# A hybrid decoder layer on one core: where DeltaNet's outputs are scaled, and when sums of weight blocks are formed

## The chip, the cores and the metric

One Trainium2 chip, one core, one launch. The metric is the device time of the launch in microseconds, the median of several executions. Everything is float32 in and out.

## The reference, cut to what matters

512 tokens of width 1024 go through two token mixers, retention and a gated DeltaNet; their outputs are merged under sigmoid gates, projected, and followed by a gated MLP with a short convolution.

```python
u = rmsnorm(h, g_mix)
rq, rk, rv, rgate, dq, dk, dv, dz, db, da, gate_r, gate_d = split(u @ w_in)
ro = groupnorm(retention_chunkwise(rotary(rq), rotary(rk) / 8, rv)) * ret_norm_g
y_ret = (silu(rgate) * ro) @ w_ret_br
q, k, v = silu(causal_dwconv([dq, dk, dv]));  q, k = l2norm(q), l2norm(k)
def step(S, (u_n, w_n, q_n, k_n, a_n, d_n)):      # chunks of 128 tokens, per head
    v_new = u_n - w_n @ S
    o = q_n @ S + a_n @ v_new
    S = S * d_n + k_n.T @ v_new
    return S, o
y_dn = (rmsnorm(scan(step)) * silu(dz)) @ w_dn_br
h = h + (sigmoid(gate_r) * y_ret + sigmoid(gate_d) * y_dn) @ w_o
a, b = split(causal_dwconv(rmsnorm(h) @ w_up) + ffn_conv_b)      # 2816 wide each
h = h + (silu(a) * b) @ w_down
return rmsnorm(h)
```

Both mixers have 8 heads; with chunks of 128 each DeltaNet head makes four steps of its scan.

## The kernel before

**Matmuls and weights.** Each product is made of three: operands are split into a high and a low part, and `mm3` adds hi x hi, hi x lo and lo x hi. SyncE fetches weights in order into four raw buffers `wraw` (`fetch`). For each block `weights` lets ACT cast `whi` and DVE subtract `wlo`; there are four buffers of each. A block's buffer comes free when it is split, so fetching goes on as ACT and DVE go on.

**Fewer products, sums of weights.** Six matrices, numbered 0 to 5 (gate_d, gate_r, w_dn_br, w_ret_br, then OUT = 4, the out projection, and DOWN = 5), are multiplied as 2 x 2 blocks with seven products instead of eight. Four of the seven take sums of weight blocks: s1 = w21 + w22, s3 = w11 + w21, s2 = w11 + s1, s4 = w12 + s2 (`SUMS`). The sums are formed in DRAM. `presum` has POOL issue, for each, one DMA that copies the first block (`s<-wm`, `s<-wd`) and later one that adds the second into it; where the second is itself a sum, its row reads `s<-s`. So s4 <- s2 may only start when s2 <- s1 has landed. `presums` spreads these DMAs over the program: for each, `pace` lets ACT write a tiny `tick`, which POOL copies to `tock`; this ties the DMA to a place in ACT's program. Each DMA of matrices 0 to 4 moves 1 MB; DOWN's are cut into four parts of 704 KB. Matrices 0 to 2 are spread over the scans; 3 and OUT follow in `late_sums`, which starts once the last head's triangular inverse is made; DOWN's 32 DMAs are spawned ahead of the out projection.

**The operands' side.** The left operands need sums too. `combine_c` makes them from `r` (or `u`, `d`): POOL subtracts into `ry`, DVE's `rz<-ry,r` and `rz<-rz,r` go on from there, then `parts_of` casts `oh` on ACT and subtracts `ol` on DVE. A matrix's results collect in `res`; POOL multiplies a finished `res` of matrix 2 by its gate (`res<-res,res`), and on matrix 3 they are transposed (`pmt`) and become the out projection's operands `mr`, `mt`, `mB`, `mT` (`m_out`; `mt1` on POOL). The residual `h` is fetched by SyncE (L1345) in eight DMAs ahead of matrix 3's weights.

**Who sets the order.** All instructions are written by one Python program in one pass, and the order of writing is the order on each engine. The class `Order` keeps a clock that each matmul moves forward (`product`), and for each engine the time at which it is free by a table of costs (`issue`). Work beside the matmuls is a generator, `spawn`ed with a delay; after each matmul `poll` resumes those whose time has come, and after its step a generator is due at the planned end of what it wrote plus `HOP` = 0.3 us. So a planned time that changes anywhere changes the order written from there on.

**The scan.** `scan` is one such generator per head. For chunk n it writes on PE `psc<-Sn,k` (state times keys), on DVE `R`, on PE `psc<-R,tt`, on ACT `vn`; on PE `psc<-vn,ktok` into quarter 3 of a PSUM bank and `psc<-Sn,q`, `psc<-vn,gb` into quarter 2 of the same bank; then on DVE the new state `Sn` from quarter 3, and on ACT the scaled output `o` from quarter 2. Four heads run in the first scan (about 190 to 275 us of the profile), four in the second (400 to 450).

After the branch matrices (to about 625 us) come the out projection, the normalised `u2`, the up projection with its convolution (products `pa`, `pb`), and from 927 us the down projection (`pd`).

Of the kernel before, what the change touches and what calls it, by code (L numbers as in the profile page):

```python
# [14 lines left out]
ALU = mybir.AluOpType  # L15
PSUM = bass.MemoryType.PSUM
# [42 lines left out]
OUT, DOWN = 4, 5  # L59
INNER = (HK, HK, HK, HK, HK, NK)  # L60
# [3 lines left out]
SUMS = (("s1", "w21", "w22"), ("s3", "w11", "w21"), ("s2", "w11", "s1"), ("s4", "w12", "s2"))  # L64
# [33 lines left out]
class Order:  # L98
# [6 lines left out]
    def __init__(self):  # L105
        self.clock = 0.0
        self.free = {}
        self.tasks = []
        self.n = 0
        self.now = None  # L110
        self.done = None

    def issue(self, engine, us):
        at = self.clock if self.now is None else self.now
        self.done = self.free[engine] = max(self.free.get(engine, 0.0), at) + us

    def product(self, us):
        self.clock += us
# [2 lines left out]
    def spawn(self, gen, after=0.0):  # L121
        self.n += 1
        heapq.heappush(self.tasks, ((self.clock if self.now is None else self.now) + after, self.n, gen))
# [41 lines left out]
class Engine:  # L165
# [7 lines left out]
    def __getattr__(self, op):  # L173
        f = getattr(self.engine, op)

        def call(out, *args, **kw):
            aps = [a for a in (*args, *kw.values()) if isinstance(a, bass.AP)]
            n = math.prod((args[0] if op == "bn_stats" else out).shape[1:])
            if op == "dma_start":
                aps = []  # L180
            ptrs = sum(a.free_size() == 1 for a in aps) if n > 1 else 0
            us = self.cost(op, n, ptrs, aps[0].space if aps else None)
            if "accum_out" in kw:
                us += 0.09 - 0.055 * (self.name == "act")
            if self.name == "vec" and any(a.tensor.name == self.last for a in aps):
                us += 0.125
            self.last = None if op == "dma_start" else out.tensor.name
            if len(args) > 1 and args[1] in TABLES and args[1] != self.table:
                self.table = args[1]
                us += 1.3  # L190
            self.order.issue(self.name, us)
            return f(out, *args, **kw)  # L192

        return call
# [19 lines left out]
def body(nc, tc, ctx, io):  # L214
    sp = nc.sync
    order = Order()
    spawn, poll, hold = order.spawn, order.poll, order.hold
    vec = Engine(order, "vec", nc.vector, vec_cost)
    act = Engine(order, "act", nc.scalar, act_cost)
    pool = Engine(order, "pool", nc.gpsimd, pool_cost)  # L220
# [10 lines left out]
    late = []  # L231
# [3 lines left out]
    def S(name, dt=F32):  # L235
        return heap.tile([P, T], dt, name=name, tag="s", bufs=HEAP)
# [4 lines left out]
    def s4(name, n=4, bufs=16):  # L241
        return mini.tile([P, n], F32, name=name, tag=f"n{n}", bufs=bufs)

    def PS(name):
        return psp.tile([P, T], F32, name=name, tag="ps")

    def v3(ap, n=4):
        return ap.rearrange("p (n f) -> p n f", n=n)

    def bc(ap, f=P):  # L250

        return ap.unsqueeze(2).to_broadcast([ap.shape[0], ap.shape[1], f])

    def ck(n, f=P):
        return slice(n * f, (n + 1) * f)
# [25 lines left out]
    sums = {(s, n): dram.tile([P, 512 * INNER[s] + 64], F32, name=f"{n}_{s}") for s in range(DOWN + 1) for n, _, _ in SUMS}  # L281

    def quarter(s, name):
        if name not in WD:
            assert (s, name) in made
            return sums[s, name]
        return (io["wd"] if s == DOWN else io["wm"][s])[WD[name]]

    made = set()

    def presum(s, parts):


        n = 512 * INNER[s] // parts
        for add in range(2):
            for name, a, b in SUMS:
                for i in range(parts):
                    c = ck(i, n)
                    kw = dict(accum_op=ALU.add) if add else {}
                    pool.dma_start(sums[s, name][:, c], quarter(s, b if add else a)[:, c],  # L300
                                        max_dma_last_dim=2048, **kw)
                    if add and i == parts - 1:
                        made.add((s, name))
                    yield

    def pace():

        tick = const.tile([P, 1], F32, name="tick", tag="tick", bufs=2)
        tock = const.tile([P, 1], F32, name="tock", tag="tock", bufs=2)
        act.copy(tick, ones[:, :1])  # L310
        pool.tensor_scalar(tock, tick, 1.0, None, ALU.mult)

    def presums(ss, parts, *times):

        todo = (None for s in ss for _ in presum(s, parts))
        for start, end, n in times:
            for i in range(n):
                while order.clock < start + (end - start) * i / n:
                    yield 0.5
                pace()  # L320
                if next(todo, 0) == 0:
                    return
                yield
# [163 lines left out]
    def rsqrt(out, ms):  # L487
        pool.tensor_tensor(out, ms, mhalf[:, :out.shape[1]], ALU.pow)
# [31 lines left out]
    def transpose4(src, name):  # L520
        pt = PS(name)
        for n in range(NT):
            pe.transpose(pt[:, ck(n)], src[:, ck(n)], ident)
        return pt
# [221 lines left out]

    spawn(clear(), 30.0)

    spawn(presums(range(3), 1, (110.0, 325.0, 24)), 30.0)
    a_dram = [dram.tile([4, GH, NT, 32, 32], F32, name=f"a_dram{g}") for g in range(2)]  # L750
    x_dram = [dram.tile([4, GH, NT, 32, 32], F32, name=f"x_dram{g}") for g in range(2)]
    R32 = [ck(b, 32) for b in range(4)]
# [170 lines left out]
    def scan(hd, i):  # L923
        h = hd["h"]
        o = S(f"o{h}")
        ssqo = s4("ssqo")
        st = None
        for n in range(NT):
            c = ck(n)
            ps = v3(PS("psc"))  # L930
            R = hd["vtok"][:, c]
            if n > 0:
                pe.matmul(ps[:, 0], hd["kT"][:, c], st, start=True, stop=True)
                yield
                R = small.tile([P, P], F32, name="R", tag="R", bufs=5)
                vec.scalar_tensor_tensor(R, ps[:, 0], hd["c2"][:, n:n + 1], hd["vtok"][:, c], ALU.mult, ALU.add)
                yield
            pe.matmul(ps[:, 1], tts[i][:, n], R, start=True, stop=True)
            yield
            vn = small.tile([P, P], F32, name="vn", tag="vn", bufs=5)  # L940
            act.copy(vn, ps[:, 1])
            yield
            if n < NT - 1:
                pe.matmul(ps[:, 3], hd["ktok"][:, c], vn, start=True, stop=True)
            if n > 0:
                pe.matmul(ps[:, 2], hd["qT"][:, c], st, start=True, stop=False)
            pe.matmul(ps[:, 2], hd["attn"][:, c], vn, start=(n == 0), stop=True)
            yield
            if n < NT - 1:
                sn = small.tile([P, P], F32, name="Sn", tag="Sn", bufs=8)  # L950
                if n == 0:
                    vec.tensor_copy(sn, ps[:, 3])
                else:
                    vec.scalar_tensor_tensor(sn, st, egl[:, h, n:n + 1], ps[:, 3], ALU.mult, ALU.add)
                st = sn
            act.activation(o[:, c], ps[:, 2], AF.Identity, scale=hd["rqs"][:, n:n + 1])
            spawn(scan_ssq(o[:, c], ssqo[:, n:n + 1]), 0.4)
            yield
        yield 0.8
        ms = s4("mso")  # L960
        vec.tensor_scalar(ms, ssqo, 1.0 / P, EPS, ALU.mult, ALU.add)
        r = s4("ro")
        yield
        rsqrt(r, ms)
        yield
        vec.tensor_tensor(v3(o), v3(o), bc(r), ALU.mult)
        hd["got"].add("o")
        yield PW
        pt = transpose4(o, "pot")
        yield  # L970
        d = S(f"doT{h}")
        act.activation(d, pt, AF.Identity, scale=prm[:, P_DG:P_DG + 1])
        doT[h] = d

    def scan_ssq(o, ssq):
        junk = small.tile([P, P], F32, name="junk", tag="junk", bufs=2)
        act.activation(junk, o, AF.Square, accum_out=ssq)
        yield
# [239 lines left out]
    def late_sums():  # L1218
        while "up" not in heads[H - 1]["got"]:
            yield 0.5  # L1220
        for s in (3, OUT):
            yield from presums((s,), 1, (order.clock, order.clock + 65.0, 8))

    for src, raw, x in ((roT, rr_, "r"), (doT, dd, "d")):
        if x == "d":
# [120 lines left out]
        matrix(s, opnd)  # L1346


    spawn(presums((DOWN,), 4, (order.clock, order.clock + 230.0, 32)))
    u2hi = [S(f"u2hi{k}", F32R) for k in range(KT)]  # L1350
    u2lo = [S(f"u2lo{k}", F32R) for k in range(KT)]
    ssqs = [s4("ssq1", 2) for _ in range(NT)]
# [49 lines left out]
    product(1, o_get, HK, [[(full, C[t], True, o_into(t, 0, C[t], ALU.add, True))] for t in range(2)])  # L1402
    product(6, o_get, HK, [[(full, A[t], False, o_into(t, 1, A[t], ALU.subtract, True))] for t in range(2)], tail=2)
    u2 = (u2hi, u2lo)


    def ffn_conv(ps, ci):
# [11 lines left out]
    f_raw, act_raw, parts = {}, {}, {}  # L1419
# [55 lines left out]
    at = [0]  # L1475
# [155 lines left out]
```

## Time and profile before

| | |
|---|---|
| median of three executions | 1037.42 us (1036.62 to 1039.86) |
| the profiled execution | 1040.07 us, span 1038.3 us, mean granted clock 0.981 |
| TensorE busy | 994.5 us, 96% |
| VectorE, ScalarE, GpSimd busy | 739.4, 536.8, 208.8 us |
| moved by DMA | 189.29 MB, 182 GB/s |

The profile is of one execution, whose own time lies 2.65 us above the median. Engines are PE (TensorE), PEld (its weight loads), DVE (VectorE), ACT (ScalarE), POOL (GpSimd) and SP (SyncE). A row such as `wlo<-wraw,whi` names what is written and from what, by the program's names. Instructions written through the recording helper all carry its line, L192 (L207 for matmuls, L211 for transposes, L274 for fetches of weights), so they are told apart by their names.

### The profile page before, as it was taken

Reading aid. Unit: us, or ns where it says so; the run is one execution under the profiler, and the core shown is the slowest. Engines: PE = TensorE matmul, PEld = TensorE weight load, DVE = VectorE, ACT = ScalarE, POOL = GpSimd, SP = SyncE. Lnnn points to the kernel's source line nnn. Section 1 sums busy time; section 2 is a strip of 40 time slices with the busy share of each in tenths; the row PEclk is TensorE's granted clock in tenths of the full one; section 3 lists DMA queues with packets and bytes.
Section 4 is the critical chain, followed back from the end, with each engine's and each line's share of the span. In section 5 each row is a group of like instructions: output and inputs, shape, how many; then the busy total and the mean of one; then the engine's idle time right before and its main releaser. Section 6 shows DMA issues by size and latency. Waiting matters only on the chain.

```text
span 1038.3 us, 14387 instructions
## 1 busy us (share of the span) xinstructions
PE 994.5 (96%) x5241; PEld 826.9 (80%) x5241; DVE 739.4 (71%) x1332; ACT 536.8 (52%) x1132; POOL 208.8 (20%) x252
## 2 busy tenths in 40 slices
PE   8999999999899999899994989999999999999997
PEld 7888888787688887778883868788888888888886
DVE  5867796665677795466787959966565576678785
ACT  5599221367645323566764545555444433346664
POOL 3022112123333122331523200231112121000001
PEclk9999999999999999999998989999999999999999
DMA  6343569747658633259997665856589988336663
GB/s 241 98 144 112 172 186 221 216 130 158 181 161 181 151 104 100 103 165 283 323 314 191 220 225 170 274 185 220 186 197 197 206 173 182 100 113 201 197 186 125
DMA packets 82230, 189.29 MB, mean 182 GB/s; under 512 B 22704, under 2 KB 31216, under 8 KB 82160
## 3 DMA queue, kind: packets, MB, share of 16 engines
q1 hardware_dynamic: 54640, 123.36, 36.3%
q0 software_dynamic: 27520, 65.02, 28.2%
q8 instruction: 41, 0.67, 0.3%
q14 instruction: 29, 0.24, 0.1%
HBM read 185.17 MB, written 68.19 MB: 244 GB/s over the span
## 4 chain that ended last, share of the span: by engine, by line
PE 83%; DVE 7%; ACT 4%; DMA 3%; issue 2%; POOL 1%; SPq 0%; POOLq 0%; DVEq 0%; ACTq 0%
PE pb L207 12%; PE pa L207 11%; PE py L207 11%; PE pd L207 10%; PE pr L207 9%; PE pz L207 8%; PE pq L207 4%; PE pv L207 4%; PE pk L207 4%; PE psc L207 2%; DVE wlo L192 2%; PE po L207 2%; DMA wraw<-s 1%; PE pm L207 1%; PE pro L207 1%
## 5 line engine op out<-in xcount | busy, mean ns | idle before, releaser
L192 DVE TENSOR_TENSOR wlo<-wraw,whi 128x1024 fp32r<-128x1024 f32 x212 | 260.0, 1229 | 70.9 <-ACT whi L192 70.4
L192 ACT CAST whi<-wraw 128x1024 fp32r<-128x1024 f32 x212 | 219.4, 1035 | 157.8 <-PE pr L207 55.9
L192 POOL TENSOR_SCALAR tock<-tick 128x1 f32<-128x1 f32 x72 | 33.3, 462 | 423.4 <-ACT tick L192 423.2
L207 PE MATMUL py<-wlo,oh 128*128 128x512 f32 x160 | 64.0, 400 | 12.3 <-DVE wlo L192 12.3
L192 DVE SCALAR_TENSOR_TENSOR acc<-pb,prm,acc 128x511 f32<-128x511 f32 (+1 forms) x44 | 33.0, 749 | 57.1 <-ACT acc L192 56.4
L207 PE MATMUL pa<-u2lo,whi 128*128 128x512 f32 (+1 forms) x192 | 71.7, 373 | 1.8 <-DVE u2lo L192 1.8
L207 PE MATMUL pa<-u2hi,whi 128*128 128x512 f32 (+1 forms) x192 | 71.6, 373 | 0.0
L207 PE MATMUL pa<-u2hi,wlo 128*128 128x512 f32 (+1 forms) x192 | 71.3, 371 | 0.0
L207 PE MATMUL pb<-u2hi,whi 128*128 128x512 f32 (+1 forms) x184 | 70.0, 380 | 0.0
L207 PE MATMUL pb<-u2lo,whi 128*128 128x512 f32 (+1 forms) x184 | 69.9, 380 | 0.0
L207 PE MATMUL pb<-u2hi,wlo 128*128 128x512 f32 (+1 forms) x184 | 69.9, 380 | 0.0
L207 PE MATMUL py<-whi,oh 128*128 128x512 f32 x160 | 64.4, 403 | 1.1 <-ACT res L192 1.1
L207 PE MATMUL py<-whi,ol 128*128 128x512 f32 x160 | 63.8, 399 | 0.0
L207 PE MATMUL pd<-whi,T 128*128 128x512 f32 (+1 forms) x198 | 55.4, 366 | 0.0
L207 PE MATMUL pz<-uhi,whi 128*128 128x512 f32 x128 | 52.5, 410 | 0.0
L207 PE MATMUL pr<-whi,uhi 128*128 128x512 f32 x128 | 51.7, 404 | 0.0
L207 PE MATMUL pz<-uhi,wlo 128*128 128x512 f32 x128 | 50.3, 393 | 0.0
L207 PE MATMUL pz<-ulo,whi 128*128 128x512 f32 x128 | 50.3, 393 | 0.0
L207 PE MATMUL pr<-whi,ulo 128*128 128x512 f32 x128 | 50.1, 391 | 0.0
L207 PE MATMUL pr<-wlo,uhi 128*128 128x512 f32 x128 | 49.9, 390 | 0.0
L192 DVE SCALAR_TENSOR_TENSOR acc<-pa,prm,acc 128x511 f32<-128x511 f32 (+1 forms) x44 | 33.0, 749 | 19.0 <-ACT acc L192 18.2
L207 PEld LDWEIGHTS py<-wlo,oh 128*128 128x128 f32 x160 | 31.0, 194 | 19.4 <-DVE wlo L192 12.7
(320 smaller groups left out, 2515.1 us busy)
## 6 DMA issues: line engine op xcount, KB each, us to landing
wraw<-w SPq DMA_DIRECT2D x100, 512.0 KB, 4.5
s<-wm POOLq DMA_DIRECT2D x30, 1024.0 KB, 8.8
wraw<-s SPq DMA_DIRECT2D x60, 512.0 KB, 4.4
s<-wd POOLq DMA_DIRECT2D x24, 704.0 KB, 5.5
wraw<-wm SPq DMA_DIRECT2D x30, 512.0 KB, 5.0
s<-s POOLq DMA_DIRECT2D x10, 1024.0 KB, 11.7
wraw<-wd SPq DMA_DIRECT2D x15, 512.0 KB, 3.7
s<-s POOLq DMA_DIRECT2D x8, 704.0 KB, 9.2
```

The source lines that it names most:

```text
L192: return f(out, *args, **kw)
L207: self.engine.matmul(out, lhsT, rhs, start=start, stop=stop, **kw)
```

## The change

It has four parts.

1. `Order.issue` is given the PSUM banks of an instruction's operands, and plans it no earlier than `HOP` after the planned end of another engine's use of the same bank. This holds for the whole program, so instructions of ACT, DVE and PE change places in many spots, each by a few rows.
2. `scan` yields between DVE's `Sn` and ACT's `o`: `o` is planned behind the state, and so is the head's next chunk.
3. `presum` takes several matrices at once. The last sum, s4 <- s2, of each is written after the first two DMAs (copies) of the next matrix, and that of the last matrix at the very end. The times follow: for matrices 0 to 2 23 DMAs over 110 to 318 us of the planner's clock and one at 330, instead of 24 over 110 to 325; in `late_sums` 15 over 125 us and one 15 us later, instead of twice 8 over 65 us.
4. DOWN's 32 sums are spawned behind the out projection, over 200 us, instead of ahead of it, over 230 us.

```diff
-    def issue(self, engine, us):
+    def issue(self, engine, us, banks=()):
         at = self.clock if self.now is None else self.now
-        self.done = self.free[engine] = max(self.free.get(engine, 0.0), at) + us
+        at = max(at, self.free.get(engine, 0.0))
+        for b in banks:
+            at = max([at, *(t + self.HOP for e, t in self.banks.get(b, {}).items() if e != engine)])
+        self.done = self.free[engine] = at + us
+        for b in banks:
+            self.banks.setdefault(b, {})[engine] = self.done
...
-            self.order.issue(self.name, us)
+            banks = {a.tensor.name for a in (out, *aps) if a.space == PSUM} if op != "dma_start" else ()
+            self.order.issue(self.name, us, banks)
...
-    def presum(s, parts):
-        n = 512 * INNER[s] // parts
-        for add in range(2):
-            for name, a, b in SUMS:
-                for i in range(parts):
-                    ...
+    def presum(ss, parts):
+        todo, late = [], []
+        for s in ss:
+            steps = [(s, name, i, q) for add in (1, 2) for name, *src in SUMS for i in range(parts) for q in (src[add - 1],)]
+            steps = [(*x, n >= len(steps) // 2) for n, x in enumerate(steps)]
+            todo += steps[:2 * parts] + late + steps[2 * parts:-parts]
+            late = steps[-parts:]
+        for s, name, i, q, add in todo + late:
+            ...
...
-    spawn(presums(range(3), 1, (110.0, 325.0, 24)), 30.0)
+    spawn(presums(range(3), 1, (110.0, 318.0, 23), (330.0, 330.0, 1)), 30.0)
...
                 st = sn
+                yield
             act.activation(o[:, c], ps[:, 2], AF.Identity, scale=hd["rqs"][:, n:n + 1])
...
-        for s in (3, OUT):
-            yield from presums((s,), 1, (order.clock, order.clock + 65.0, 8))
+        c = order.clock
+        yield from presums((3, OUT), 1, (c, c + 125.0, 15), (c + 140.0, c + 140.0, 1))
...
-    spawn(presums((DOWN,), 4, (order.clock, order.clock + 230.0, 32)))
...
     product(6, o_get, HK, [[(full, A[t], False, o_into(t, 1, A[t], ALU.subtract, True))] for t in range(2)], tail=2)
     u2 = (u2hi, u2lo)
+    spawn(presums((DOWN,), 4, (order.clock, order.clock + 200.0, 32)))
```

The number of instructions of each kind stays as it was. Three places show what moves. The first is POOL during matrix 2, where OUT's last two sums were issued. `s_4_95` and `s_4_96` are OUT's s2 and s4 in both programs; before, the rows are

```order
L192 DMA s_4_95<-s_4_93 128x4x512
L192 TENSOR_TENSOR ry_5596<-r_3871,r_3693 128x256
L192 TENSOR_TENSOR ry_5596<-r_3693 128x256
L192 TENSOR_SCALAR tock<-tick 128x1
L192 DMA s_4_96<-s_4_95 128x4x512
L192 TENSOR_TENSOR ry_5622<-r_3913,r_3743 128x256
L192 TENSOR_TENSOR ry_5646<-r_3953,r_3787 128x256
L192 TENSOR_TENSOR ry_5622<-r_3743 128x256
L192 TENSOR_TENSOR res_5568<-res_5568,res_4834 128x512
L192 TENSOR_TENSOR ry_5646<-r_3787 128x256
L192 TENSOR_TENSOR res_5573<-res_5573,res_4845 128x512
L192 TENSOR_TENSOR ry_5669<-r_3995,r_3829 128x256
```

and now

```order
L200 TENSOR_SCALAR tock<-tick 128x1
L200 DMA s_4_95<-s_4_93 128x4x512
L200 TENSOR_TENSOR ry_5639<-r_3789 128x256
L200 TENSOR_TENSOR ry_5666<-r_3997,r_3831 128x256
L200 TENSOR_TENSOR res_5568<-res_5568,res_4845 128x512
L200 TENSOR_TENSOR ry_5666<-r_3831 128x256
L200 TENSOR_TENSOR res_5743<-res_5743,res_4976 128x512
L200 TENSOR_TENSOR res_5751<-res_5751,res_4981 128x512
L200 TENSOR_TENSOR res_5691<-res_5691,res_4934 128x512
L200 TENSOR_TENSOR res_5696<-res_5696,res_4939 128x512
L200 TENSOR_SCALAR tock<-tick 128x1
L200 DMA s_4_96<-s_4_95 128x4x512
```

The last sum, `s_4_96<-s_4_95`, stood with only two `ry` between it and the sum that it reads; all the other `ry` and `res` stood behind it. Now the `ry` and `res` stand ahead of it, and it comes after the last `res` pair.

The second is the place of that last sum's `tick` on ACT, during matrix 2's last products. Before, ACT had there

```order
L192 CAST oh<-ry_5646 128x512
L192 CAST whi<-wraw 128x1024
L192 CAST oh<-ry_5669 128x512
L192 CAST whi<-wraw 128x1024 x5
L192 ACTIVATE res_5950<-py 128x512
L192 ACTIVATE res_5955<-py 128x512
L192 CAST whi<-wraw 128x1024 x3
L192 COPY mr_6022<-pmt 128x512
L192 CAST mB_6029<-mr_6022 128x512
```

and now it has

```order
L200 CAST oh<-ry_5639 128x512
L200 CAST whi<-wraw 128x1024
L200 CAST oh<-ry_5666 128x512
L200 CAST whi<-wraw 128x1024 x2
L200 COPY tick<-ones 128x1
L200 CAST whi<-wraw 128x1024 x3
L200 ACTIVATE res_5950<-py 128x512
L200 ACTIVATE res_5955<-py 128x512
L200 CAST whi<-wraw 128x1024 x3
L200 COPY mr_6022<-pmt 128x512
L200 CAST mB_6029<-mr_6022 128x512
```

The `tick` of the last sum has come between the second and the third of five casts of weights; the casts themselves keep their order.

The third is DVE in the first scan, at the last states of heads 2 and 3 (`Sn`), with the retention's `ro` and `sT`. Before:

```order
L192 SCALAR_TENSOR_TENSOR k_2482<-pk,prm,k_2482 128x509
L192 TENSOR_SCALAR ro<-pro,mv,rgn 128x128 x4
L192 TENSOR_TENSOR wlo<-wraw,whi 128x1024
L192 TENSOR_TENSOR sT<-prs,cst 128x512 x2
L192 TENSOR_TENSOR o_2124<-o_2124,ro 128x512
L192 SCALAR_TENSOR_TENSOR Sn<-Sn,egl,psc 128x128 x2
L192 COPY rS<-pkv 128x128
L192 SCALAR_TENSOR_TENSOR R<-psc,c_1032,vtok_1168 128x128
L192 SCALAR_TENSOR_TENSOR R<-psc,c_1208,vtok_1301 128x128
```

Now:

```order
L200 SCALAR_TENSOR_TENSOR Sn<-Sn,egl,psc 128x128
L200 TENSOR_SCALAR ro<-pro,mv,rgn 128x128 x4
L200 TENSOR_SCALAR ssk<-ssk 128x4
L200 TENSOR_SCALAR ro<-pro,mv,rgn 128x128 x4
L200 TENSOR_TENSOR sT<-prs,cst 128x512 x2
L200 TENSOR_TENSOR c_2610<-beta,rk 128x4
L200 TENSOR_TENSOR sr<-c_2610,rk 128x4
L200 SCALAR_TENSOR_TENSOR c_2611<-sr,eG 128x4
L200 SCALAR_TENSOR_TENSOR A_2523<-pkk,sr,gb_2269 128x128 x4
L200 SCALAR_TENSOR_TENSOR R<-psc,c_1032,vtok_1168 128x128
L200 COPY rS<-pkv 128x128
L200 SCALAR_TENSOR_TENSOR Sn<-Sn,egl,psc 128x128
```

The two `Sn` stood as a pair behind `ro`, `wlo`, `sT` and the normalised outputs `o`; now one stands ahead of `ro` and the other behind `ro`, `sT` and the first instructions of head 4's `A`, close behind its `R`.

More of the change, by code (lines that the diff above doesn't have):

```diff
@@ L107, in __init__ @@
         self.free = {}
+        self.banks = {}
         self.tasks = []
@@ L289, in body @@
     made = set()
-    def presum(s, parts):
-        n = 512 * INNER[s] // parts
-        for add in range(2):
-            for name, a, b in SUMS:
-                for i in range(parts):
[L298 to L304, printed above, removed]
+    def presum(ss, parts):
[6 more added lines that the diff above has]
+        for s, name, i, q, add in todo + late:
+            c = ck(i, 512 * INNER[s] // parts)
+            kw = dict(accum_op=ALU.add) if add else {}
+            pool.dma_start(sums[s, name][:, c], quarter(s, q)[:, c], max_dma_last_dim=2048, **kw)
+            if add and i == parts - 1:
+                made.add((s, name))
+            yield
     def pace():
@@ L313, in presums @@
     def presums(ss, parts, *times):
-        todo = (None for s in ss for _ in presum(s, parts))
+        todo = presum(ss, parts)
         for start, end, n in times:
@@ L955, in scan @@
                 st = sn
+                yield
             act.activation(o[:, c], ps[:, 2], AF.Identity, scale=hd["rqs"][:, n:n + 1])
```

## The prediction

> **What bounds the kernel now.** I read the page first: which engine is full, and what the chain that ended last is made of.
>
> ```profile
> PE 994.5 (96%) x5241; PEld 826.9 (80%) x5241; DVE 739.4 (71%) x1332; ACT 536.8 (52%) x1132; POOL 208.8 (20%) x252
> PE 83%; DVE 7%; ACT 4%; DMA 3%; issue 2%; POOL 1%; SPq 0%; POOLq 0%; DVEq 0%; ACTq 0%
> ```
>
> TensorE is busy for 994.5 of 1038.3 us. The change takes no matmul away, so only the other 43.8 us, and the stretches in which TensorE runs at a lower clock, can give time. So the waits of PE come next: who was waited for, us in total, times, the longest.
>
> ```profile
> PE py L207 <- DVE wlo L192: 12.3, 1, 12.3
> PE psc L207 <- DVE Sn L192: 5.4, 3, 3.1
> PE pmt L211 <- DVE res L192: 3.9, 1, 3.9
> PE pvt L211 <- ACT v L192: 3.1, 1, 3.1
> PE po L207 <- DVE wlo L192: 2.3, 1, 2.3
> PE psc L207 <- DVE R L192: 2.0, 2, 1.4
> ```
>
> One wait of 12.3 us is the largest by far; the three rows of the scans make 10.5 us. Third, busy time and granted clock around each, to see what a wait leaves behind it (columns: window, its length, busy us and count of PE, PEld, DVE, ACT, POOL, then PE's clock, the DMA engines' busy share, GB/s).
>
> ```profile
> 235.40:240.40 5.00, 4.81 (x22) 4.28 (x23) 1.31 (x5) 4.77 (x13) 0.00 (x0) 0.66 0.50 179
> 266.00:271.00 5.00, 5.00 (x33) 3.71 (x34) 4.47 (x9) 4.40 (x10) 1.02 (x2) 0.66 0.81 149
> 430.00:435.00 5.00, 4.62 (x20) 4.15 (x21) 1.92 (x8) 2.97 (x13) 0.61 (x2) 0.66 0.23 93
> ...
> 558.10:570.40 12.30, 0.03 (x1) 0.00 (x0) 9.00 (x7) 3.12 (x5) 7.85 (x9) 0.62 0.54 97
> 570.40:575.00 4.60, 4.57 (x12) 3.62 (x13) 4.57 (x7) 2.37 (x5) 0.00 (x0) 0.54 0.61 195
> 575.00:602.80 27.80, 27.80 (x123) 22.71 (x121) 21.30 (x22) 12.11 (x15) 7.05 (x4) 1.00 0.74 259
> 602.80:606.70 3.90, 0.04 (x1) 0.00 (x0) 3.71 (x6) 2.21 (x3) 0.00 (x0) 0.82 0.56 184
> 606.70:612.10 5.40, 5.35 (x16) 4.38 (x17) 4.16 (x5) 1.99 (x3) 0.00 (x0) 0.50 0.54 163
> ```
>
> A wait costs twice: itself, and the clock after it. After the 12.3 us it stands at 0.54 over 4.60 us (4.60 x 0.46 = 2.1 us lost), after the 3.9 us at 0.50 over 5.40 (2.7), in the three scan windows at 0.66 over 5.00 (1.7 each, about 1.5 in the last, which holds some idle time: 4.9). So 14.4 us are at stake at 570 and 15.4 in the scans.
>
> **The sums of the matrices.** Fourth, what ended the 12.3 us: the rows of POOL, DVE and PE there (start, duration, what, and the idle time before with its releaser).
>
> ```profile
> 542.36 1.30 POOL L192 DMA_DIRECT2D s<-s  x1 [0.37 <-issue]
> ...
> 548.92 0.21 POOL L192 TENSOR_SCALAR tock<-tick 128x1 f32<-128x1 f32 x1 [3.79 <-ACT tick L192]
> ...
> 559.24 1.30 POOL L192 DMA_DIRECT2D s<-s  x1 [10.10 <-DMA wraw<-s]
> 560.07 1.90 POOL L192 TENSOR_TENSOR ry<-r,r 128x256 f32<-128x256 f32 x2
> ...
> 565.91 1.18 POOL L192 TENSOR_TENSOR ry<-r 128x256 f32<-128x256 f32 x1
> ```
>
> ```profile
> 561.33 6.05 DVE L192 SCALAR_TENSOR_TENSOR rz<-ry,r 128x256 f32<-128x256 f32 x1 [7.23 <-POOL ry L192]
> 567.42 0.42 DVE L192 SCALAR_TENSOR_TENSOR rz<-rz,r 128x256 f32<-128x256 f32 x1
> ...
> 569.15 1.22 DVE L192 TENSOR_TENSOR wlo<-wraw,whi 128x1024 fp32r<-128x1024 f32 x1
> ```
>
> OUT's last sum, s4 <- s2, stands next on POOL at 548.92, but reads s2, whose own second half was issued at 542.36; it goes out at 559.24, 16.9 us later. (The named releaser, a transfer of SyncE, is only the last one that the profile saw; the sum has no need of it.) Behind it, in order, stand `ry` and `res`; DVE's `rz` waits for the `ry`, `wlo` stands behind `rz`, and PE waits for `wlo`. The change moves this sum far back: on POOL its place falls behind all of these, so the wait on s2 is gone (s2 has then had some 49 us). I take the whole 14.4 us away and ask what is late next. DVE's `rz` took 6.05 us where its twin took 0.42, while POOL's `ry` and `res` ran. That POOL work stays and now runs from about 549; DVE has wlo, two `ol`, a `res` to do before it. Residual: nothing if POOL is done by then, 3.5 us if `rz` is blocked in one piece of a few POOL instructions; I take 1.5, nearer to nothing, since they start 10 us earlier.
>
> By the Trainium skill ("SBUF — State Buffer", section "SBUF: two separate sides") the pair of ports that VectorE shares with GpSimd is an exclusive lock whose loser blocks for whole instructions. The 6.05 us beside 0.42 agree; the rule speaks against this change, since the POOL work is only moved and blocks wherever it lands: by it I would put 3.5 in place of 1.5, and the sum 2 us higher.
>
> Where does the sum go? On ACT its `tick` now stands between two `whi` casts, those that ran at 585.65 and 588.37, and on POOL behind the last `res` pair:
>
> ```profile
> 587.10 3.52 POOL L192 TENSOR_TENSOR res<-res,res 128x512 f32<-128x512 f32 x2 [2.97 <-DVE res L192]
> ```
>
> ```profile
> 588.37 1.06 ACT L192 CAST whi<-wraw 128x1024 fp32r<-128x1024 f32 x1 [1.67 <-PE py L207]
> ...
> 601.87 2.17 ACT L192 CAST whi<-wraw 128x1024 fp32r<-128x1024 f32 x2 [6.03 <-DMA wraw<-s]
> ```
>
> ```profile
> 589.92 3.88 SPq L1345 DMA_DIRECT2D h<-x  x8
> 594.11 14.07 SPq L274 DMA_DIRECT2D wraw<-s  x6
> ...
> 622.77 0.33 SPq L274 DMA_DIRECT2D wraw<-s  x1
> ```
>
> So it is issued at about 591 of the old time: exactly when SyncE fetches the eight `h`, and just ahead of the weights for which ACT already waited 6.03 us, DVE's `res` behind it, and PE 3.9 us. Its price: in a quieter window two such accumulating transfers moved 2.10 MB (first row) and took 74.2% of 16 engines over 17 us, 12.6 us, so 6.3 us for one of 1 MB; by the queue's mean over the kernel (28.2% of 1038.3 us for 65.02 MB, 4.5 us a MB) it is 4.7. The third row is how long such a sum takes to land.
>
> ```profile
> q0 software_dynamic: 1056, 2.10, 74.2%
> ```
>
> ```profile
> q0 software_dynamic: 27520, 65.02, 28.2%
> s<-s POOLq DMA_DIRECT2D x10, 1024.0 KB, 11.7
> ```
>
> Between 0 (the transfer stretches and leaves the engines to the weights) and +6.3 (all of it ahead of the weights) I take +4.7, since the weights there were late already. SyncE wants s4 itself only for the second product on OUT, whose first fetch goes out at 622.77 (last row of SyncE above); landing 11.7 us after 591, or 20 in the crowd, it is there. The sums of the first three matrices move too, with nothing of PE behind POOL there: 0.
>
> **The scans.** ACT's `o` now stands behind DVE's `Sn` in the plan, and the planner knows of banks. On the chip much of this already held:
>
> ```profile
> ACT o L192 <- DVE Sn L192: 24.4, 16, 6.2
> ```
>
> In 16 of 24 steps `o` waited for `Sn` anyway. What moves is who waits behind `o` (ACT's `vn`, casts and `k`), and how the scan's matmuls fall between the others. The longest wait, ended by this row, comes from DVE's order: the last `Sn` of heads 2 and 3 stand as a pair behind `wlo`, `sT` and `o`.
>
> ```profile
> 233.40 1.29 DVE L192 TENSOR_TENSOR sT<-prs,cst 128x512 f32<-128x512 f32 x2
> 234.59 0.69 DVE L192 TENSOR_TENSOR o<-o,ro 128x512 f32<-128x512 f32 x1
> 235.19 0.61 DVE L192 SCALAR_TENSOR_TENSOR Sn<-Sn,egl,psc 128x128 f32<-128x128 f32 x2
> ```
>
> In the new order one of them comes ahead of `ro` and `sT`, the other behind them. That place is worth 3.1 + 1.7 = 4.8; I take -4. The ends: all 15.4 away, or +5, one such place more. For the 2.0 and 3.1 us of the other rows I see the same instructions ahead as before (`uz` ahead of `Sn` at 430, `gb` ahead of `v`), so they stay.
>
> The windows of 430 and 235 show the clock falling after waits of at most 2.3 (5.4 less 3.1) and 3.1 us. By the Trainium skill ("TensorE: Matmul & The Clock Gate", section "What's actually happening") it falls after an idle window of about 3.4 us that runs freely; the shorter waits here were followed by the lower clock all the same, so the rows decide; by the rule the place would be worth 3.1 instead of 4.8.
>
> **The out and the down projection.** DOWN's sums start behind the out projection: eight transfers of 704 KB leave it, and the two `mt` of POOL run earlier. PE's 2.3 us there follow this:
>
> ```profile
> 648.84 3.40 DVE L192 SCALAR_TENSOR_TENSOR mt<-mt,mr 128x512 f32<-128x512 f32 x1
> ```
>
> DVE's `mt` took 3.40 us beside POOL's. The block moves with POOL's `mt`; DVE is full there and the weights are not what PE waits for. Taken as 0, with -2.3 (the wait gone) and +2.3 (another as long) as ends. In the up projection all 32 fall into 200 us instead of 230 us begun earlier:
>
> ```profile
> 687.17:926.88 239.71, 239.71 (x1123) 201.23 (x1122) 151.56 (x221) 98.78 (x157) 36.16 (x51) 1.00 0.69 174
> ```
>
> PE has no gap at all there and the DMA engines are 0.69 busy; eight more transfers of 0.72 MB at 4.5 us a MB are 26 us of 240, so 0.80. Free: the cover is that share below 1 and the buffers of weights ahead. If it went, PE would wait for `whi`.
>
> The bank rule also moves a few instructions at the start and shifts the last transposes of `u2` behind about nine matmuls: +0.5, between -1.9 and +1.9, which is nine times the 0.21 us of a matmul in the row above (239.71 us over 1123).
>
> **The sum.** Against the profiled execution, 1040.07 us (span 1038.3): -14.4 + 1.5 + 4.7 - 4 + 0 + 0.5 = -11.7, so 1028.4. That execution lies 2.65 above the median 1037.42 of the three runs, which I take off: 1025.7.
>
> **Rivals.** (1) Given back: the residual is 3.5, the late sum costs 6.3 and the scans nothing: -14.4 + 3.5 + 6.3 + 0.5 = -4.1, so 1033.3. For it: the DMA engines' crowd at 591 and POOL's block. Beside it stands a rule of the Trainium skill ("DMA: Bandwidth & Descriptors", section "SWDGE vs HWDGE vs iDMA"): every DMA engine takes turns between the software and the hardware queue, so the sum would get its half at once; only the run can show it. (2) Hidden: residual and collision 0, the scans give back half of 15.4: -14.4 - 8 = -22.4, so 1015.0. For it: s4 is wanted only 31 us later, and a transfer behind a full queue may simply stretch. (3) The scans' part does nothing, since ACT waited anyway: -7.7, so 1029.7. (4) Slower: with the planner putting each scan's next matmul and `o` later, the chain of a head grows. If `o`, 0.37 us, comes into each of 24 steps, that is 8.9 us, and two more halved windows make 12.3; with the -7.7 of the rest, +4.6, so 1042.0. It decides once the scans lose over 10.8 us (7.7 and the bound of 3.1). Against it: PE has other matmuls between the scans' steps.
>
> **How the numbers follow.** 0.3%, about what a measurement of this kernel can tell from no change, is 3.1 us: faster is below 1034.3, slower above 1040.5. Forecast 0.42, rival 3 0.15, rival 1 0.15 (a fifth of it beyond 1034.3), rival 2 0.17, rival 4 0.06, an unforeseen small loss 0.05, mostly within 0.3%. So faster 0.84, same 0.09, slower 0.07. The range runs from rival 2, 1014, to just past rival 1, 1035, and leaves out 0.2. The forecast's own range is 1021 to 1029.
>
> **What would show it.** PE's row "py <- DVE wlo" falls from 12.3 to under 4; the releaser of POOL's last `s<-s` is a tick, and nothing waits behind it; ACT's wait for `wraw<-s` near 590 grows from 6.0 to 8 to 12 us, PE's "pmt <- DVE res" with it; the scan rows fall from 10.5 to about 7; the up projection stays without gaps. It is wrong if the 12.3 us go to another wait of the branch matrices, if the scans' rows grow, or if PE waits for `whi` in the up projection.

## The result: 1028.16 us, and the profile after

The changed kernel takes 1028.16 us (median of four, 1027.78 to 1029.33) against 1037.39: a ratio of 0.9909, 95% interval 0.989 to 0.9927. The forecast was 1025.7. The profiled execution took 1027.94 us with a span of 1026.1; before it was 1040.07, so the two profiles are 12.1 us apart and the medians 9.2. The sum was made between profiles and came to -11.7.

The sum came out nearly right, and its terms did not. The waits of PE after the change (who was waited for, us in total, times, longest):

```profile
PE pmt L219 <- DVE res L200: 8.8, 1, 8.8
PE py L215 <- DVE wlo L200: 7.2, 2, 5.5
PE pm L215 <- DMA tt<-x_dram: 2.5, 1, 2.5
...
PE psc L215 <- DVE R L200: 1.7, 2, 1.2
```

The 12.3 us are gone, but 7.2 us of the same wait stay, and the wait for `res` has grown from 3.9 to 8.8: the two together were 16.2 us and are 16.0. Of the scans' 10.5 us only 1.7 are left, and a wait of 2.5 us for the transfer `tt<-x_dram` is new. To see what each stage is worth, take the first and last start of groups of PE's matmuls, the last two numbers before the semicolon; first the kernel before, then after.

```profile
L207 PE MATMUL pz<-uhi,whi x128: 387/390/774, 335.1 to 457.2; 128*128 128x512 f32 x128
L207 PE MATMUL py<-whi,oh x160: 388/389/775, 468.8 to 634.3; 128*128 128x512 f32 x160
L207 PE MATMUL po<-whi,mT x64: 387/389/629, 647.8 to 681.5; 128*128 128x512 f32 x64
L207 PE MATMUL pd<-whi,T x198: 278/389/398, 956.6 to 1031.7; 128*128 128x512 f32 x154, 128*128 128x256 f32 x44
```

```profile
L215 PE MATMUL pz<-uhi,whi x128: 388/390/504, 332.0 to 448.1; 128*128 128x512 f32 x128
L215 PE MATMUL py<-whi,oh x160: 387/390/775, 460.3 to 623.5; 128*128 128x512 f32 x160
L215 PE MATMUL po<-whi,mT x64: 387/390/506, 637.3 to 668.3; 128*128 128x512 f32 x64
L215 PE MATMUL pd<-whi,T x198: 278/389/398, 944.4 to 1019.5; 128*128 128x512 f32 x154, 128*128 128x256 f32 x44
```

Start and first scan, to the first `pz`: 335.1 to 332.0, -3.1 us. The second scan, first to last `pz`: 122.1 to 116.1, -6.0. The branch matrices, last `pz` to last `py`: 177.1 to 175.4, -1.7. The out projection, last `py` to last `po`: 47.2 to 44.8, -2.4. From there to the last `pd`: 350.2 to 351.2, +1.0. The matrices, where the change to the sums aims, gave only 1.7 us.

**What is left of the 12.3 us.** POOL and DVE where the stall was, after the change:

```profile
548.08 1.24 POOL L200 TENSOR_TENSOR ry<-r 128x256 f32<-128x256 f32 x1
548.77 1.23 POOL L200 TENSOR_TENSOR ry<-r,r 128x256 f32<-128x256 f32 x1
549.45 1.76 POOL L200 TENSOR_TENSOR res<-res,res 128x512 f32<-128x512 f32 x1
550.67 1.22 POOL L200 TENSOR_TENSOR ry<-r 128x256 f32<-128x256 f32 x1
```

```profile
548.20 4.79 DVE L200 TENSOR_TENSOR wlo<-wraw,whi 128x1024 fp32r<-128x1024 f32 x1
...
554.29 1.22 DVE L200 TENSOR_TENSOR wlo<-wraw,whi 128x1024 fp32r<-128x1024 f32 x1
```

POOL no longer waits for the sum there. It computes until 551.89, and the `wlo` that PE wants lasts 4.79 us, from POOL's first `ry` to just behind its last, instead of 1.22. The shorter of the two waits, 1.7 us, follows a `wlo` of the same kind: 4.87 us at 536.86, beside five `ry` of POOL.

**Where the sum went.** ACT, POOL, SyncE and PE around the fetch of `h` (issued from 575.07 to 578.98), and how long the transfers of this window took to land:

```profile
591.58 1.04 ACT L200 CAST whi<-wraw 128x1024 fp32r<-128x1024 f32 x1 [10.87 <-DMA wraw<-s]
```

```profile
576.89 1.30 POOL L200 DMA_DIRECT2D s<-s  x1
```

```profile
575.07 3.91 SPq L1357 DMA_DIRECT2D h<-x  x8
```

```profile
596.46 1.11 PE L219 MATMUL pmt<-cst,res 128*128 128x128 f32 x4 [8.76 <-DVE res L200]
```

```profile
wraw<-s SPq DMA_DIRECT2D x6, 512.0 KB, 12.6
h<-x SPq DMA_DIRECT2D x8, 256.0 KB, 5.8
s<-s POOLq DMA_DIRECT2D x1, 1024.0 KB, 15.6
```

ACT's wait for weights grew from 6.03 to 10.87 us and PE's from 3.91 to 8.76. The sum itself is issued at 576.89, in the middle of the fetch of `h`.

### The profile page after: what moved, and what is told of

Read it like the earlier page. It is cut to its first block, busy times and chain, and to the rows that moved or that the text cites. A ratio compares the mean times of both kernels' runs of the same rounds, so it can differ in the third digit from the quotient of the medians.

```text
span 1026.1 us, 14395 instructions
## 1 busy us (share of the span) xinstructions
PE 991.8 (97%) x5241; PEld 823.5 (80%) x5241; DVE 737.7 (72%) x1332; ACT 535.6 (52%) x1132; POOL 213.9 (21%) x252
## 4 chain that ended last, share of the span: by engine, by line
PE 59%; DVE 8%; DMA 4%; ACT 3%; issue 2%; POOL 0%; POOLq 0%; DVEq 0%; ACTq 0%
PE pa L215 12%; PE pb L215 12%; PE pd L215 10%; PE pz L215 8%; PE py L215 5%; DVE wlo L200 3%; DMA wraw<-s 3%; PE pv L215 2%; PE po L215 2%; PE pq L215 2%; DMA wraw<-wm 2%; PE psc L215 1%; PE pk L215 1%; DVE res L200 1%; ACT whi L200 1%
## 5 line engine op out<-in xcount | busy, mean ns | idle before, releaser
L200 DVE TENSOR_TENSOR wlo<-wraw,whi 128x1024 fp32r<-128x1024 f32 x212 | 267.6, 1265 | 71.0 <-ACT whi L200 70.6
L200 POOL TENSOR_SCALAR tock<-tick 128x1 f32<-128x1 f32 x72 | 35.6, 495 | 356.1 <-ACT tick L200 356.0
L215 PEld LDWEIGHTS pa<-u2lo,whi 128*128 128x128 f32 x192 | 36.2, 188 | 8.7 <-DVE u2lo L200 2.4
```

The costliest lines, as they stand in the source:

```text
L215: self.engine.matmul(out, lhsT, rhs, start=start, stop=stop, **kw)
```

## The experiments

Ratios are to the kernel before, run on the same chip at the same time.

**Each part of the change alone: e1 to e4.** e1 has only the `yield` in `scan`:

```diff
                 st = sn
+                yield
             act.activation(o[:, c], ps[:, 2], ...)
```

> The kernel before with the yield between the state and the scaled output alone (part 2). Theory: the scans' gain needs the bank rule and the yield together, so the yield alone gives about a third of the 9 us: 1034, with PE's waits for Sn and R falling from 7.4 us to about 4. Rival: ACT waited for Sn anyway, so 1037, and the wait rows stay.

Measured: ratio 0.9935 (0.9911 to 0.996), so 6.7 us less, about twice what was expected. PE's waits for `Sn` and `R` are gone in its profile, and the wait for `wlo` stays at 11.8 us.

e2 has only the bank rule in `Order`:

```diff
-            self.order.issue(self.name, us)
+            self.order.issue(self.name, us, banks)
```

> The kernel before with the planner's bank rule alone (part 1). Theory: most of what the scans gained, about 5 us, so 1032, the 12.3 us wait of the branch matrices unchanged. Rival: the rule only shuffles rows, 1036 to 1039.

Measured: 0.9897 (0.9862 to 0.9933), as much as the whole change.

e3 has both of these edits:

> Parts 1 and 2 together, sums as before. Theory: the scans' whole gain of about 8 us, so 1029, with the 12.3 us wait of the branch matrices still there. Rival: the scans gained because the sums' transfers moved, so 1036 or more here.

Measured: 0.9903 (0.9868 to 0.9939), near the 1029 us expected, and the wait for `wlo` is still there (9.6 us the longest). The rule and the `yield` together give no more than the rule alone.

e4 has only the new order and times of the sums of matrices 0 to 4, with the new `presum`:

```diff
-    spawn(presums(range(3), 1, (110.0, 325.0, 24)), 30.0)
+    spawn(presums(range(3), 1, (110.0, 318.0, 23), (330.0, 330.0, 1)), 30.0)
...
-        for s in (3, OUT):
-            yield from presums((s,), 1, (order.clock, order.clock + 65.0, 8))
+        c = order.clock
+        yield from presums((3, OUT), 1, (c, c + 125.0, 15), (c + 140.0, c + 140.0, 1))
```

> The new order and times of the sums of matrices 0 to 4 alone (part 3). Theory: the branch matrices alone gain, about 2 us (12.3 us and its slow clock gone, 5 to 7 us back as DVE blocked beside POOL, 5 us back at the fetch of h), so 1035; the scans' waits as before. Rival: the moved transfers also help the scans, 1030.

Measured: 0.998 (0.9956 to 1.0003): the 2 us expected, but not to be told from no change.

So the bank rule alone gives what the whole change gives. The `yield` alone gives some of it too, and the gains do not add. That another new order would have done as much as the rule's is not excluded. The expectation of e2 gave the scans 5 us and was short; it failed in place, since its 12.3 us are not "unchanged". With the sums in their old order, the rule alone brings PE's wait for `wlo` down:

```profile
PE pmt L219 <- DVE res L200: 4.5, 1, 4.5
PE py L215 <- DVE wlo L200: 3.6, 1, 3.6
```

POOL in e2 shows why: the `ry` and `res` are now written ahead of the sum's `tick`, all but one, so that little hangs on the sum's wait. The sum still goes out only 15.3 us behind the one that it reads (first row), as it did 16.9 us behind it in the kernel before.

```profile
539.57 1.30 POOL L200 DMA_DIRECT2D s<-s  x1 [0.23 <-issue]
...
549.68 1.71 POOL L200 TENSOR_TENSOR ry<-r,r 128x256 f32<-128x256 f32 x1
551.37 0.66 POOL L200 TENSOR_SCALAR tock<-tick 128x1 f32<-128x1 f32 x1
554.84 1.30 POOL L200 DMA_DIRECT2D s<-s  x1 [2.82 <-issue]
555.67 1.24 POOL L200 TENSOR_TENSOR ry<-r 128x256 f32<-128x256 f32 x1
```

In e3, where the `yield` moves the order once more, the `ry` stand behind the sum again, and the chain of before is back: POOL, DVE and PE.

```profile
554.05 1.30 POOL L200 DMA_DIRECT2D s<-s  x1 [8.47 <-issue]
```

```profile
556.14 4.71 DVE L200 SCALAR_TENSOR_TENSOR rz<-ry,r 128x256 f32<-128x256 f32 x1 [5.71 <-POOL ry L200]
```

```profile
562.50 0.80 PE L215 MATMUL py<-wlo,oh 128*128 128x512 f32 x1 [9.59 <-DVE wlo L200]
```

Yet e3's matrices take 175.1 us, and those of the changed kernel, where part 3 has moved the sum away, 175.4. In e2 they take 169.0; but the profile of e2 is of its fastest execution (1023.64 us, median 1028.0), and that of e3 of one of its slower ones (1030.94, median 1029.48).

The scans tell the same. From first to last `pz` the second scan takes 122.1 us before, and 115.4, 113.7, 116.0 and 117.8 us in e1 to e4: every new order is better than the old one, even e4, which does not touch the code of the scan. And the wait that the `yield` is about is not what costs. ACT's wait of `o` for `Sn`, 24.4 us before, is this in the changed kernel and in e2:

```profile
ACT o L200 <- DVE Sn L200: 13.0, 8, 3.7
```

```profile
ACT o L200 <- DVE Sn L200: 26.0, 16, 6.1
```

e2 has the longest of these waits and the shortest second scan. In e4 the first scan is slower instead: its first `pz` starts at 341.2, against 335.1 before; that took away more than the 5.5 us which its matrices gained (177.1 to 171.6).

**The collision: e5 and e6.** Both start from the changed kernel. e5 has the last sum earlier:

```diff
-        yield from presums((3, OUT), 1, (c, c + 125.0, 15), (c + 140.0, c + 140.0, 1))
+        yield from presums((3, OUT), 1, (c, c + 125.0, 15), (c + 130.0, c + 130.0, 1))
```

> The changed kernel with OUT's last sum 10 us earlier in the planner's clock (130 instead of 140 us behind the start of the late sums), so that it is issued some 12 to 15 us before the eight fetches of h. Theory: the collision is the sum's; PE's wait for res falls from 8.8 to about 4 us and the time by 5 us with it, to 1023.5. Rival: h and the weights crowd each other anyway, and the wait stays above 7 us: 1028.

Measured: 0.9888 (0.9855 to 0.9921). The sum is issued at 566.90, 10.8 us ahead of the fetch of `h`, and PE's wait for `res` halves:

```profile
PE pmt L219 <- DVE res L200: 4.3, 1, 4.3
```

The matrices take 171.0 us instead of 175.4, so 4.4 us less, as expected; the whole gained less (2 us by the ratios, inside their intervals). In this profile the first `pz` came at 334.3 instead of 332.0, in a stretch whose program is the same, and the stretch behind the out projection took 352.5 us instead of 351.2.

e6 leaves the sum where it is and spreads the fetch of `h`:

```diff
         if s == 3:
             for t in range(NT):
                 for i in range(2):
                     h1[t][i] = S(f"h1_{t}{i}")
-                    sp.dma_start(h1[t][i], xv[t, :, ck(i, T)])
+            def h_loads():
+                for t in range(NT):
+                    for i in range(2):
+                        sp.dma_start(h1[t][i], xv[t, :, ck(i, T)])
+                        yield 3.0
+            spawn(h_loads(), 15.0)
```

> The changed kernel with the eight fetches of h spread over matrix 3, one each 3 us of the planner's clock, instead of all ahead of its weights; SyncE's order alone changes. Theory: 2 MB leave the place where the sum runs, the weights come some 5 to 6 us earlier, PE's wait for res falls from 8.8 to 2 to 4 us: 1022. Rival: the sum alone holds the weights back: wait above 6 us, 1026 or more.

Measured: 0.9817 (0.9781 to 0.9853), 1018.85 us; the best single step of the study. PE and ACT there:

```profile
PE pmt L219 <- DVE res L200: 1.0, 1, 1.0
```

```profile
588.73 1.05 ACT L200 CAST whi<-wraw 128x1024 fp32r<-128x1024 f32 x1 [5.04 <-DMA wraw<-s]
```

The sum is still there, issued at 577.34, and ACT still waits 5.04 us for weights; but PE now waits 1.0 us and has no slow clock after it. So the sum alone costs PE 1.0 us of waiting (e6), `h` alone 3.9 (the kernel before) or 4.3 (e5), and both at once 8.8, more than the two added. That blocks of weights already split cover the first part of ACT's wait would explain this, but was not tested.

**POOL beside DVE: e7.** The changed kernel, with `ry` of matrix 3's operands on DVE:

```diff
-        pool.tensor_tensor(t3, b22, b12, ALU.subtract)
+        eng = vec if x == "r" else pool
+        eng.tensor_tensor(t3, b22, b12, ALU.subtract)
         yield
-        pool.tensor_tensor(t1, b11, b12, ALU.subtract)
+        eng.tensor_tensor(t1, b11, b12, ALU.subtract)
```

> The changed kernel with the eight subtractions ry of matrix 3's operands on DVE instead of POOL. Theory: the two waits for wlo (1.7 and 5.5 us, and the slow clock behind) come from DVE held up while POOL computes; without POOL's ry the wlo there take 1.2 us each instead of 4.8, the waits fall to under 2 us together: 1022. Rival: DVE is simply short of time there, eight subtractions of 0.4 us more lengthen the waits: 1029 to 1031.

Measured: 0.9887 (0.9855 to 0.9919). By the ratios that is 2 us less than the change, inside their intervals. Both theories hold in part: the wait for `wlo` falls from 7.2 to 2.7 us, and the next wait takes part of it.

```profile
PE pmt L219 <- DVE res L200: 10.5, 1, 10.5
...
PE py L215 <- DVE wlo L200: 2.7, 1, 2.7
```

On DVE seven of the eight `ry` take 0.42 us each, and the `wlo` there 1.22; what is left of the block is one `ry` beside POOL's remaining `res`:

```profile
545.18 1.22 DVE L200 TENSOR_TENSOR wlo<-wraw,whi 128x1024 fp32r<-128x1024 f32 x1
546.31 3.48 DVE L200 TENSOR_TENSOR ry<-r,r 128x256 f32<-128x256 f32 x1
```

That is the lock which the Trainium skill names ("SBUF — State Buffer", "SBUF: two separate sides"): the trace agrees, 4.79 us beside POOL's work and 1.22 without it. In this trace the wait lasts over four instructions of POOL in a row.

**DOWN's sums: e8.** The changed kernel with DOWN's sums spawned ahead of the out projection again (part 4 undone):

```diff
+    spawn(presums((DOWN,), 4, (order.clock, order.clock + 230.0, 32)))
     u2hi = [S(f"u2hi{k}", F32R) for k in range(KT)]
...
     u2 = (u2hi, u2lo)
-    spawn(presums((DOWN,), 4, (order.clock, order.clock + 200.0, 32)))
```

> The changed kernel with DOWN's sums started ahead of the out projection again (part 4 undone). Theory: the out projection, between the last matmuls of the branch matrices and its own, takes 47.2 us again instead of 44.8, and the stretch from there to the end 1.0 us less: 1029.5. Rival: the 2.4 us came from the new order of the rows, and 1028 stays.

Measured: 0.9921 (0.9894 to 0.9947), 1.2 us more than the change, by the ratios within their intervals, but with the stages as expected: last `py` to last `po` 47.1 us instead of 44.8, and from there to the first `pa` 0.5 instead of 1.6.

```profile
L215 PE MATMUL py<-whi,oh x160: 389/389/776, 461.3 to 624.2; 128*128 128x512 f32 x160
L215 PE MATMUL po<-whi,mT x64: 387/389/507, 637.6 to 671.3; 128*128 128x512 f32 x64
L215 PE MATMUL pa<-u2hi,whi x192: 278/389/389, 671.8 to 910.4; 128*128 128x512 f32 x160, 128*128 128x256 f32 x32
```

**Together, and the rest told apart: e9 to e12.** e9 has e6 and e7 together.

> The changed kernel with both h spread over matrix 3 and ry on DVE. Theory: two separate costs, so the gains add: the waits for wlo fall as with ry alone (7.2 to 2.7 us, and their slow clock), the wait for res as with h alone (to 1 us): 1018.9 less 4 is 1014 to 1015. Rival: what ry gives is only handed on to the next transfer, as it was with h in the crowd: 1018 or more.

Measured: 0.9789 (0.9765 to 0.9813). Against e6's 0.9817 that is about 3 us less, within the intervals. The wait for `wlo` fell to 2.3 us and the one for `res` rose from 1.0 to 4.7. The matrices take 167.3 us, and 166.7 in e6: in this stage the rival held, and the gain was handed on.

e10 is the kernel before with `h` spread, as in e6.

> The kernel before with h spread over matrix 3 and nothing else. Theory: without the late sum beside it the fetch of h costs the 3.9 us wait and 2.7 us of slow clock, so 6 us less than before: 1031 to 1032. Rival: h hurts only together with the late sum: within 2 us of before.

Measured: 0.9956 (0.9932 to 0.998), 4.6 us less by the ratio, nearer to the theory's 6 than to the rival. The wait for `res` is gone; 1.4 us came back in the wait for `wlo`, which is 13.7 us there instead of 12.3. So the fetch of `h` had a price without the late sum too.

e11 is e6 with the sums of matrices 0 to 4 in their old order (part 3 undone).

> The changed kernel with h spread and the sums of matrices 0 to 4 in their old order (part 3 undone). Theory: without the collision the new order of the sums is worth what the stall behind POOL takes, 4 to 7 us: 1024, against 1018.9 with it. Rival: the bank rule alone already frees the place, and part 3 is worth nothing even here: 1019.

Measured: 0.9813 (0.979 to 0.9835), against e6's 0.9817. The rival held in the time: part 3 is worth nothing that can be seen, even where nothing collides. Part 3 does shorten the stall a little, which is longer without it:

```profile
PE py L215 <- DVE wlo L200: 9.1, 2, 8.3
```

That is 1.7 us more than e6's 7.4, and e11 has no 1.0 for `res`; the matrices take 166.9 us there and 166.7 in e6.

e12 is e9 without the `yield` (part 2 undone).

> The changed kernel with h spread, ry on DVE and without the yield in the scan (part 2 undone). Theory: beside the bank rule, which plans o behind the state anyway since both read one bank, the yield is worth nothing: within 2 us of the same kernel with it. Rival: the yield is part of the scans' gain: 3 to 5 us more than with it.

Measured: 0.9745 (0.9719 to 0.9772), 1012.53 us, and neither theory: without the `yield` it is about 5 us faster than with it (medians 1012.53 and 1017.68; the two intervals overlap by 0.0007). It is the fastest kernel here, at a ratio of 0.9745 where the changed one has 0.9909. Its page and its largest wait in the matrices:

```profile
PE 986.6 (98%) x5241; PEld 820.5 (81%) x5241; DVE 734.6 (73%) x1340; ACT 535.4 (53%) x1132; POOL 201.4 (20%) x244
```

```profile
PE pmt L219 <- DVE res L200: 2.6, 1, 2.6
```

Of the 9.8 us between its profile and e9's, 7.1 lie in the matrices (160.2 us instead of 167.3), where PE waits 0.5 us for `wlo` and 2.6 for `res`; in e9 it waits 2.3 and 4.7, and 0.3 for another `res`. The profiles overstate the step, since e12's is of its fastest execution and e9's of one of its slowest. Why the order without the `yield` suits the matrices better was not tried; e2 and e3, which differ by the `yield` as well, point the same way.

## Why the prediction was right, and where its terms were not

The total came out by luck. The prediction names as a sign of being wrong that the 12.3 us go to another wait of the branch matrices, and they did: the waits for `wlo` and `res` were 16.2 us and are 16.0. What made up for it was the scans, which gave more than twice their term.

**The residual of the stall: this step was wrong.** The 14.4 us went, as worked out, but "nearer to nothing, since they start 10 us earlier" was not so: 7.2 us of waits and 1.6 of slow clock stayed (4.90 us at 0.68, first row below), where 1.5 stood in the sum, and even the end of its range was 3.5. It counted POOL's blocks on one `rz`; the block fell on whichever DVE instruction was next, and most of it on the `wlo` that PE wanted. e7 shows it: with POOL's `ry` away, 7.2 became 2.7.

```profile
553.10:558.00 4.90, 4.90 (x15) 3.92 (x16) 4.83 (x9) 2.09 (x3) 0.00 (x0) 0.68 1.00 259
...
596.40:600.90 4.50, 4.44 (x13) 3.69 (x14) 4.17 (x6) 1.20 (x2) 0.00 (x0) 0.53 0.44 147
```

**The late sum: right in place and size.** +4.7 stood there; the wait grew by 4.85 us (3.91 to 8.76), its slow clock fell from 2.7 to 2.1 (4.50 at 0.53, second row above). e5 took 4.4 of it back by moving the sum, e6 took nearly all by moving `h`. But that price is not the sum's own, since beside a spread `h` it costs 1.0. What was missed is that the fetch of `h`, not the sum, was the better thing to move.

**The scans: the sign right, the size short.** -4 stood there; the first scan with the start gave 3.1 and the second 6.0. The step that failed is "I see the same instructions ahead as before", from which the other rows were to stay: `uz` (423.01) does stand ahead of `Sn` (424.93) still, but PE has other matmuls to run meanwhile and is busy for 5.00 of the 5.00 us from 421 to 426. It needs no one part: e1 to e4 each shorten the second scan by 4 to 8 us, e2 without the `yield` and e1 without the rule. Which single row of the order cost the old one its stalls was not tried. The sums of matrices 0 to 2 stood at 0 as well, and that was not quite so: PE's new wait for `tt<-x_dram` (2.5 us) is in the profile of every run with part 3 and of none without it, and these transfers take 5.1 us to land where they took 2.8.

**The out projection and the rest.** 0 stood there for the out projection, with -2.3 as an end; it gave 2.4. POOL's `mt` do run earlier (at 625.74, before at 649.15), and DVE had room for the block there, which the term denied. The +0.5 for `u2` came as +1.1, but with part 4, not the bank rule: e8 has the rule and 0.5 us between `po` and `pa`, the changed kernel 1.6. The up projection stayed without gaps, but for the two waits for `u2lo` at its start (1.8 us together, before too).

So -8.2 for the matrices was -1.7, -4 for the scans was -9.1, and the rest, +0.5, was -1.4; together -12.2 in place of -11.7. Two errors of 5 to 7 us cancelled. Rival 1 comes nearer in the matrices (-4.6), rival 2 in the scans (-8).

The 2.65 us taken off for the slow profile of before moved the forecast away from the measured 1028.16; without them it was 1028.4. The terms had been priced in that slow profile. The stages add up to 12.2 us between two profiles, but the medians lie only 9.2 apart, so some 3 us belong to that one execution and not to the change. They hardly lie in the scans: e10, whose program is the same up to the matrices, has its first `pz` at 335.5 and a second scan of 122.2 us. Where they lie is open.

## What to carry to other kernels

Where order is made by a planner, one rule in it moves rows everywhere, and a term for one place is not a term for the change: compare stages by the first and last start of their matmuls, and run each part alone before crediting it. A transfer moved out of a stall should go where no burst is waiting; look for the one that is there already, since moving the burst (e6) may be worth more than moving the newcomer. And work taken off a stalled POOL still blocks DVE when it runs: count its whole length against the DVE instruction that PE waits for next.

## What the hardware showed that was not expected

A wait of PE well under 3 us can be followed by half clock. In e9 this is the stretch after a wait of 2.32 us (columns as above, the clock ahead of the last two); after a wait of 1.67 us in the changed kernel, the second row, the clock stayed at 1.00:

```profile
548.80:551.80 3.00, 2.95 (x7) 2.37 (x8) 2.97 (x7) 1.90 (x3) 0.00 (x0) 0.50 1.13 206
...
541.78:547.50 5.72, 5.72 (x24) 4.43 (x24) 5.65 (x9) 2.41 (x5) 2.23 (x3) 1.00 1.10 260
```

And stretches whose program is the same vary by up to 2.3 us between profiles: the first `pz` started at 332.0, 334.3, 332.2, 333.8, 333.0 and 332.5 in the changed kernel and in e5 to e9. A single profile can't tell a term of that size, and the 3.1 us of the start and the first scan are little more.
